# The last feed-forward of a hybrid trunk: block sums made in place, three steps begun ahead, fetches of hid in slots of their own

## The chip, the cores and the metric

One core of a Trainium2 chip runs the whole trunk in one launch. The metric is device time in microseconds (us): the median of several runs. One further execution is recorded by the hardware profiler; all rows of a profile come from it. Engines: PE is TensorE (matmul), PEld its weight loads, DVE is VectorE, ACT is ScalarE, POOL is GpSimd, SP is SyncE, which here only issues DMAs.

## The reference

Two layers of a mixing block (attention and a state-space scan) and a SwiGLU feed-forward, over 256 context and 1024 latent tokens, D_MODEL = 1024, float32. Only the feed-forward of the last layer is touched:

```python
f_l = rmsnorm(x_lat, norm_ffn_pre[l]) * (1.0 + sc2_l) + sh2_l
x_lat = x_lat + g2_l * rmsnorm(swiglu(f_l, w_gate[l], w_up[l], w_down[l]), norm_ffn_post[l])

def swiglu(h, w_gate, w_up, w_down):
    return (jax.nn.silu(h @ w_gate) * (h @ w_up)) @ w_down
```

In the last layer it is computed for the 1024 latent tokens alone. D_FF is 2816, 22 steps (`ff`) of 128.

## The kernel before

**Products.** Every float32 operand is held as a pair: hi, a rounded cast made on ACT (line 113), and lo, the difference made on POOL or DVE (line 114). `mm3` (lines 227 to 230) multiplies them in three matmuls of 128 x 128 x 512.

**The last feed-forward** (`ffn_last`) makes gate and up of one step together as a 2 x 2 block product with seven instead of eight multiplications (Strassen's scheme in Winograd's form). The weights' blocks of a step are A11, A12 (the halves of the gate's rows), A22 (a half of the up rows), and the sums S1 = u0 + u1, S2 = S1 - g0, S3 = g0 - u0, S4 = g1 - S2. The tokens' blocks are B11, B21, B22 and T1 to T4, made once by `quads` from the normalised tokens; B11 and B21 (tile `ha`) are there from the first half of the tokens, the others (`h_hb` holds T1 and T2, `h_hc` B22, `h_t` T3 and T4) need the second half, token tiles 6 to 9. One block's product is 12 matmuls, a step is 84. `head(ff)` makes A11·B11 and A12·B21, which need only `ha`; `rest(ff)` the other five, the sums in between on DVE, and stores the two halves of the hidden rows through an xt tile to DRAM (`hid`, line 1032).

**Weights.** `plan` lists the blocks in the order in which they are used, two to a ring slot `w_t`, five slots; `pump` fills a slot as soon as the one five places back is freed by TensorE. `wblock` (lines 201 to 224) makes one block: it fetches the step's gate or up weights (512 KB, line 208) into one of two raw slots (`raw_t`), makes the four sums (lines 217 to 220) into two xt tiles, and splits. Heads 0 and 1 are made before the second half of the tokens is there, so the gate weights of steps 0 and 1 are fetched twice. xt is a pool of six tiles of 128 x 1024 that tokens, quadrants, sums and hid share.

**The down projection** (`down_all`) takes the token tiles in groups of three, three and two (`GROUPS`), and for each group goes through all 22 steps: one weight block of 512 KB (line 124, cast and split as above, through the same raw slots and ring) and the hid rows of the group (line 1081, an xt tile of its own), 18 matmuls a step in the first two groups and 12 in the third. hid is fetched three steps ahead. A group's sums stay in PSUM (slots `ps_w`, five, and `ps_s`, three, of a bank each); at its end `finish_psum` and `postnorm` (lines 796 to 801) normalise them, add the residual, in xt tiles, and store.

**Order.** A scheduler, not the code's order alone, sets each engine's row of instructions when the kernel is built; at run time each engine goes through its own row in order and waits at an instruction until its operands and slots are there. SP issues all fetches of weights, tokens and hid in one row.

Of the kernel before, what the change touches and what calls it, by code (L numbers as in the profile page):

```python
# [9 lines left out]
F32 = mybir.dt.float32  # L10
F32R = mybir.dt.float32r
AF = mybir.ActivationFunctionType
ALU = mybir.AluOpType
# [4 lines left out]
P = 128  # L18
# [6 lines left out]
NCT = CTX // P  # L25
# [4 lines left out]
NFF = DFF // P  # L30
# [24 lines left out]
class Trunk:  # L55
# [73 lines left out]
    def plan(self):  # L129
# [15 lines left out]
        for l in range(DEPTH):  # L145
# [8 lines left out]
            if l == 1:  # L154
                flat = [(ff, b) for ff in range(2) for b in ("A11", "A12")]
                flat += [(ff, b) for ff in range(2) for b in ("S2", "S3", "S1", "A22", "S4")]
                flat += [(ff, b) for ff in range(2, NFF) for b in ("A11", "A12", "S2", "S3", "S1", "A22", "S4")]
# [42 lines left out]
    def wblock(self, w, ff, name):  # L200
# [11 lines left out]
        if name[0] == "S" and "S1" not in st:  # L212
            u = raw("u")
            a, b = self.x(), self.x()
            st["S1"], st["S2"], st["S3"], st["S4"] = a[:, 0:512], a[:, 512:1024], b[:, 0:512], b[:, 512:1024]
            add = nc.vector.tensor_tensor
            add(st["S1"], u[:, 0:512], u[:, 512:1024], op=ALU.add)
            add(st["S2"], st["S1"], g[:, 0:512], op=ALU.subtract)
            add(st["S3"], g[:, 0:512], u[:, 0:512], op=ALU.subtract)
            add(st["S4"], g[:, 512:1024], st["S2"], op=ALU.subtract)  # L220
        src = st[name] if name[0] == "S" else {"A11": g, "A12": g, "A22": st.get("u")}[name][:, 512 * (name != "A11"):512 * (name != "A11") + 512]
        self.split(w[:, 0], w[:, 1], src, nc.gpsimd)
        if name == ("A12" if ff < 2 else "S4"):
            st.clear()
# [736 lines left out]
    def quads(self, xs, i, B):  # L961
# [4 lines left out]
        for k2 in range(0, 4, 2):  # L966
# [13 lines left out]
            t3 = self.s2()  # L980
# [8 lines left out]
            tt(t3, b22, b12, op=ALU.subtract)  # L989
            tt(b12, b12, b11, op=ALU.subtract)  # L990
            put("T1", b12, nc.gpsimd)
            tt(b22, b22, b12, op=ALU.subtract)
            put("T2", b22, nc.vector)
            put("T3", t3, nc.vector)
            tt(b22, b22, b21, op=ALU.subtract)
            put("T4", b22, nc.gpsimd)

    def ffn_last(self, l, accp, xs0, xs1):
# [19 lines left out]

        def head(ff):
            a, x1, sa = self.psw(), self.s2(), self.s2()  # L1020
# [13 lines left out]
        def rest(ff):  # L1034
# [17 lines left out]
            p = self.psw()  # L1052
            mul(p, ff, "S4", "B22")
# [8 lines left out]
        self.quads(xs1, 1, B)  # L1062
        for ff in range(NFF):
            if ff > 1:
                head(ff)
            rest(ff)
        self.down_all(l)

    def down_all(self, l):
        nc = self.nc  # L1070
        loads = [(g, ff) for g in range(len(self.GROUPS)) for ff in range(NFF)]
        hx = {}

        def load(n):
            if n < len(loads):
                g, ff = loads[n]
                ts = self.GROUPS[g]
                w = len(ts) * P
                a = self.x(n=2 * w)
                o = (ts[0] - NCT) * P  # L1080
# [3 lines left out]
        for n in range(3):  # L1084
            load(n)
# [248 lines left out]
```

## Time and profile before

| what | value |
|---|---|
| runs | 3324.96, 3329.06, 3329.13 us, median 3329.06 |
| profiled execution | 3319.59 us, its span on the core 3317.8 |
| mean granted clock | 0.969 |
| last feed-forward, TensorE's part | from about 2564 to 3307 us of the span |
| down projection | from about 3034 to 3307 us |

The profiled execution is 9.5 us (0.28 %) shorter than the median of the runs. In rows of the profile "L208" is line 208 of the kernel, "raw_t<-in_w_up" the tile written and what is read, a number with x a count, and what stands in square brackets the idle time of the engine just ahead with what ended it.

### The profile page before, as it was taken

Reading aid. Unit: us, or ns where it says so; the run is one execution under the profiler, and the core shown is the slowest. Engines: PE = TensorE matmul, PEld = TensorE weight load, DVE = VectorE, ACT = ScalarE, POOL = GpSimd, SP = SyncE. Lnnn points to the kernel's source line nnn. Section 1 sums busy time; section 2 is a strip of 40 time slices with the busy share of each in tenths; the row PEclk is TensorE's granted clock in tenths of the full one; section 3 lists DMA queues with packets and bytes.
Section 4 is the critical chain, followed back from the end, with each engine's and each line's share of the span. In section 5 each row is a group of like instructions: output and inputs, shape, how many; then the busy total and the mean of one; then the engine's idle time right before and its main releaser. Section 6 shows DMA issues by size and latency. Waiting matters only on the chain. (4 is left out here: it accounts for less than half of the span.)

```text
span 3317.8 us, 44735 instructions
## 1 busy us (share of the span) xinstructions
PE 3097.4 (93%) x16411; PEld 2564.5 (77%) x16411; DVE 1722.2 (52%) x3188; ACT 1338.4 (40%) x2440; POOL 1546.7 (47%) x1429
## 2 busy tenths in 40 slices
PE   6999989999899999989999998889999699999997
PEld 4777768888777788866778787778887488887785
DVE  2657567765343344436334467677775655663000
ACT  4433347666422121134222354347675433332222
POOL 4226455444433223246344525644546655554665
PEclk8999889999999999999999999999999799999998
DMA  6376553221343322244444335752222333335766
GB/s 223 100 220 231 175 169 102 64 64 64 118 124 96 102 78 70 64 144 150 139 140 127 109 87 163 236 157 83 71 64 91 114 113 108 106 112 181 239 219 215
DMA packets 327082, 434.08 MB, mean 131 GB/s; under 512 B 22408, under 2 KB 236584, under 8 KB 326608
## 3 DMA queue, kind: packets, MB, share of 16 engines
q1 hardware_dynamic: 266976, 340.26, 33.5%
q10 hardware_dynamic: 59888, 90.97, 7.5%
q8 instruction: 130, 2.13, 0.3%
q14 instruction: 88, 0.72, 0.1%
HBM read 340.14 MB, written 91.01 MB: 130 GB/s over the span
## 5 line engine op out<-in xcount | busy, mean ns | idle before, releaser
L114 POOL TENSOR_TENSOR w_t<-raw_t,w_t 128x1024 fp32r<-128x1024 f32 (+2 forms) x288 | 619.5, 2156 | 916.2 <-ACT w_t L113 892.1
L113 ACT CAST w_t<-raw_t 128x1024 fp32r<-128x1024 f32 (+2 forms) x314 | 296.3, 949 | 682.0 <-PE ps_s L230 203.1
L1146 DVE TENSOR_TENSOR ffn_acc<-ffn_acc,ps_s 128x512 f32<-128x512 f32 x400 | 270.8, 685 | 201.0 <-PE ps_s L230 199.4
L848 DVE TENSOR_SCALAR_CACHE_REDUCE att_a<-ps_s 128x512 f32<-128x512 f32 (+1 forms) x400 | 226.9, 586 | 138.6 <-PE ps_s L847 128.2
L856 POOL TENSOR_SCALAR att_a<-att_a,att_st 128x1280 f32<-128x1280 f32 (+1 forms) x144 | 180.2, 1253 | 176.1 <-DVE att_st L855 109.5
L113 ACT CAST xt<-s2t 128x512 fp32r<-128x512 f32 (+2 forms) x148 | 80.6, 545 | 353.8 <-DVE s2t L1127 201.3
L228 PE MATMUL ps_s<-w_t,xt 128*128 128x512 f32 x528 | 211.6, 401 | 12.0 <-ACT xt L113 4.2
L1127 DVE TENSOR_TENSOR s2t<-s2t,ps_w 128x256 f32<-128x256 f32 (+1 forms) x66 | 39.4, 597 | 334.2 <-PE ps_w L230 318.5
L228 PE MATMUL ps_w<-ha,w_t 128*128 128x512 f32 x528 | 207.2, 394 | 1.9 <-ACT xt L979 1.1
L229 PE MATMUL ps_w<-ha,w_t 128*128 128x512 f32 x528 | 207.1, 393 | 1.7 <-DVE ha L387 1.7
L230 PE MATMUL ps_s<-w_t,xt 128*128 128x512 f32 x528 | 206.1, 393 | 1.5 <-DVE xt L114 1.5
L229 PE MATMUL ps_s<-w_t,xt 128*128 128x512 f32 x528 | 207.4, 393 | 0.0
L230 PE MATMUL ps_w<-ha,w_t 128*128 128x512 f32 x528 | 206.7, 392 | 0.0
L869 PE MATMUL ps_w<-cst_all,att_a 128*128 128x128 f32 x1312 | 198.5, 277 | 0.3 <-DVE xt L799 0.2
L854 ACT ACTIVATE att_a<-att_a,att_st 128x1280 f32<-128x1280 f32 (+1 forms) x144 | 183.2, 1273 | 37.2 <-DVE att_st L853 32.3
L114 POOL TENSOR_TENSOR w_t<-xt,w_t 128x512 fp32r<-128x512 f32 x88 | 127.3, 1457 | 111.4 <-ACT w_t L113 111.4
L799 DVE SCALAR_TENSOR_TENSOR xt<-ps_w,rstd_t,gate_row 128x512 f32<-128x512 f32 x48 | 33.6, 745 | 278.3 <-POOL rstd_t L236 278.2
L869 PEld LDWEIGHTS ps_w<-cst_all,att_a 128*128 128x128 f32 x1312 | 154.4, 142 | 11.3 <-DVE xt L799 5.4
L465 DVE SCALAR_TENSOR_TENSOR xt<-row,convw,xt 128x512 f32<-128x512 f32 (+1 forms) x128 | 126.4, 1041 | 68.8 <-ACT xt L463 51.3
L114 DVE TENSOR_TENSOR xt<-s2t,xt 128x512 fp32r<-128x512 f32 (+2 forms) x148 | 129.8, 877 | 49.3 <-ACT xt L113 47.9
L228 PE MATMUL ps_w<-hb,w_t 128*128 128x512 f32 x352 | 140.9, 400 | 0.8 <-ACT s2t L382 0.8
L229 PE MATMUL ps_w<-hb,w_t 128*128 128x512 f32 x352 | 139.5, 396 | 0.0
(334 smaller groups left out, 8551.5 us busy)
## 6 DMA issues: line engine op xcount, KB each, us to landing
raw_t<-in_w_down SPq DMA_DIRECT2D x110, 512.0 KB
raw_m<-in_w_mod SPq DMA_DIRECT2D x80, 512.0 KB
raw_t<-in_w_gate SPq DMA_DIRECT2D x68, 512.0 KB
raw_t<-in_w_up SPq DMA_DIRECT2D x66, 512.0 KB
hid<-xt ACTq DMA_DIRECT2D x44, 512.0 KB
xt<-xs SPq DMA_DIRECT2D x42, 512.0 KB
xt<-hid SPq DMA_DIRECT2D x44, 384.0 KB
raw_t<-in_w_in SPq DMA_DIRECT2D x32, 512.0 KB
```

The lines of the kernel that those rows point to most:

```text
L113: self.nc.scalar.copy(hi, src)
L114: (eng or self.nc.vector).tensor_tensor(lo, src, hi.bitcast(F32), op=ALU.subtract)
L228: mm(out, st[0], mv[0], start=first, stop=False)
L229: mm(out, st[0], mv[1], start=False, stop=False)
L230: mm(out, st[1], mv[0], start=False, stop=last)
L465: nc.vector.scalar_tensor_tensor(acc, row[:, o0 + k:o0 + k + n], cw[:, ct, k:k + 1], acc, op0=ALU.mult, op1=ALU.add)
L848: nc.vector.tensor_scalar(pb[:, j:j + m], s[:, :m], -0.125, None, op0=ALU.mult, op1=ALU.min, accum_out=st[:, n:n + 1])
L854: nc.scalar.activation(pb, pb, AF.Exp, bias=nmx, scale=-1.0, accum_out=st[:, 4:5])
L856: nc.gpsimd.tensor_scalar(pb, pb, st[:, 5:6], 1.0, op0=ALU.mult, op1=ALU.mult)
L869: nc.tensor.transpose(tp[:, (2 * k + h) * P:(2 * k + h + 1) * P], pr[h][:, (k2 + k) * P:(k2 + k + 1) * P], self.ident)
L1127: nc.vector.tensor_tensor(s, s, ps["u"][:, :n], op=ALU.mult)
L1146: nc.vector.tensor_tensor(acc[t][:, s], acc[t][:, s], p, op=ALU.add)
```

## The change

Three parts, all in the last feed-forward.

- **Sums in place.** S1 is written over u's first half, S2 and S4 over g's halves, and only S3 goes to a tile of its own (an s2 tile). No xt tile is used, but a gate slot is held until S2 and S4 are split, an up slot until S1 and A22 are. In `quads` the differences are made over B11, B12, B22 and B21; T1's lo is made on DVE and T3's on POOL, where it was the other way round.
- **Three steps begun.** head(2) stands ahead of the steps too, in two tiles of another pool, so the gate weights of step 2 are fetched a second time as well. Of step 0 the product S4·B22 is made first (`third`), copied to a tile x3 by ACT, and used later.
- **Fetches of hid.** The first three go to xt tiles and are issued ahead of the last step's `rest`; the others go to a ring of ten places in the space of `ha`, nine steps ahead.

The diff:

```diff
--- before.py
+++ after.py
@@ -152,9 +152,9 @@
             for kt in range(self.RING):
                 seq.append(((l, "o", kt), [(slice(0, 1024), I["w_out"][l][kt * P:(kt + 1) * P, :].unsqueeze(1))], (1, 1024)))
             if l == 1:
-                flat = [(ff, b) for ff in range(2) for b in ("A11", "A12")]
-                flat += [(ff, b) for ff in range(2) for b in ("S2", "S3", "S1", "A22", "S4")]
-                flat += [(ff, b) for ff in range(2, NFF) for b in ("A11", "A12", "S2", "S3", "S1", "A22", "S4")]
+                flat = [(ff, b) for ff in range(3) for b in ("A11", "A12")]
+                flat += [(ff, b) for ff in range(3) for b in (("S4",) if ff == 0 else ()) + ("S2", "S3", "S1", "A22") + (("S4",) if ff else ())]
+                flat += [(ff, b) for ff in range(3, NFF) for b in ("A11", "A12", "S2", "S3", "S1", "A22", "S4")]
                 self.wpos = {b: (i // 2, i % 2) for i, b in enumerate(flat)}
                 for i in range(0, len(flat), 2):
                     seq.append(((l, "w", i // 2), flat[i:i + 2], None))
@@ -211,16 +211,15 @@
         g = raw("g") if name in ("A11", "A12") or "S1" not in st else None
         if name[0] == "S" and "S1" not in st:
             u = raw("u")
-            a, b = self.x(), self.x()
-            st["S1"], st["S2"], st["S3"], st["S4"] = a[:, 0:512], a[:, 512:1024], b[:, 0:512], b[:, 512:1024]
+            st["S1"], st["S2"], st["S3"], st["S4"] = u[:, 0:512], g[:, 0:512], self.s2(), g[:, 512:1024]
             add = nc.vector.tensor_tensor
-            add(st["S1"], u[:, 0:512], u[:, 512:1024], op=ALU.add)
-            add(st["S2"], st["S1"], g[:, 0:512], op=ALU.subtract)
             add(st["S3"], g[:, 0:512], u[:, 0:512], op=ALU.subtract)
-            add(st["S4"], g[:, 512:1024], st["S2"], op=ALU.subtract)
+            add(st["S1"], st["S1"], u[:, 512:1024], op=ALU.add)
+            add(st["S2"], st["S1"], st["S2"], op=ALU.subtract)
+            add(st["S4"], st["S4"], st["S2"], op=ALU.subtract)
         src = st[name] if name[0] == "S" else {"A11": g, "A12": g, "A22": st.get("u")}[name][:, 512 * (name != "A11"):512 * (name != "A11") + 512]
         self.split(w[:, 0], w[:, 1], src, nc.gpsimd)
-        if name == ("A12" if ff < 2 else "S4"):
+        if name == ("A22" if ff == 0 else "S4") or name == "A12" and ff < 3:
             st.clear()
 
     def mm3(self, out, st, mv, first, last):
@@ -977,7 +976,6 @@
                     kt = k2 + 4 * half + k
                     o = half * 512 + k * 256
                     nc.scalar.activation(qb[:, o:o + 256], t[:, k * 256:(k + 1) * 256], AF.Identity, bias=cc[:, kt:kt + 1], scale=cc[:, 16 + kt:17 + kt])
-            t3 = self.s2()
             b11, b21, b12, b22 = qa[:, 0:512], qa[:, 512:1024], qb[:, 0:512], qb[:, 512:1024]
 
             def put(name, src, eng):
@@ -986,14 +984,14 @@
                 eng.tensor_tensor(d[:, :, 1], v(src), d[:, :, 0].bitcast(F32), op=ALU.subtract)
 
             put("B22", b22, nc.gpsimd)
-            tt(t3, b22, b12, op=ALU.subtract)
-            tt(b12, b12, b11, op=ALU.subtract)
-            put("T1", b12, nc.gpsimd)
-            tt(b22, b22, b12, op=ALU.subtract)
+            tt(b11, b12, b11, op=ALU.subtract)
+            tt(b12, b22, b12, op=ALU.subtract)
+            tt(b22, b22, b11, op=ALU.subtract)
             put("T2", b22, nc.vector)
-            put("T3", t3, nc.vector)
-            tt(b22, b22, b21, op=ALU.subtract)
-            put("T4", b22, nc.gpsimd)
+            put("T3", b12, nc.gpsimd)
+            put("T1", b11, nc.vector)
+            tt(b21, b22, b21, op=ALU.subtract)
+            put("T4", b21, nc.gpsimd)
 
     def ffn_last(self, l, accp, xs0, xs1):
         nc = self.nc
@@ -1016,8 +1014,16 @@
         tt = nc.vector.tensor_tensor
         st = {}
 
+        def third(ff):
+            p = self.psw()
+            mul(p, ff, "S4", "B22")
+            x3 = accp.tile([P, 512], F32, name="x3")
+            nc.scalar.copy(x3, p)
+            st["x3"] = x3
+
         def head(ff):
-            a, x1, sa = self.psw(), self.s2(), self.s2()
+            x1, sa = [accp.tile([P, 512], F32, name=f"head{i}") if ff == 2 else self.s2() for i in range(2)]
+            a = self.psw()
             mul(a, ff, "A11", "B11")
             nc.scalar.copy(x1, a)
             a = self.psw()
@@ -1049,8 +1055,11 @@
             tt(u3, u3, p, op=ALU.subtract)
             tt(sa, sa, u3, op=ALU.mult)
             emit_hid(sa, ff, 0)
-            p = self.psw()
-            mul(p, ff, "S4", "B22")
+            if ff == 0:
+                p = st["x3"]
+            else:
+                p = self.psw()
+                mul(p, ff, "S4", "B22")
             tt(u2, u2, p, op=ALU.add)
             nc.scalar.activation(u2, u2, AF.Silu)
             tt(u2, u2, x1, op=ALU.mult)
@@ -1060,28 +1069,44 @@
         self.quads(xs0, 0, B)
         head(1)
         self.quads(xs1, 1, B)
+        head(2)
+        third(0)
         for ff in range(NFF):
-            if ff > 1:
+            if ff > 2:
                 head(ff)
+            if ff == NFF - 1:
+                hx, load = self.hid_loader()
+                for n in range(3):
+                    load(n)
             rest(ff)
-        self.down_all(l)
-
-    def down_all(self, l):
-        nc = self.nc
-        loads = [(g, ff) for g in range(len(self.GROUPS)) for ff in range(NFF)]
-        hx = {}
+        self.down_all(l, hx, load)
+
+    def hid_loader(self):
+        self.loads = loads = [(g, ff) for g in range(len(self.GROUPS)) for ff in range(NFF)]
+        hx, ring = {}, []
 
         def load(n):
-            if n < len(loads):
-                g, ff = loads[n]
-                ts = self.GROUPS[g]
-                w = len(ts) * P
+            if n >= len(loads):
+                return
+            g, ff = loads[n]
+            ts = self.GROUPS[g]
+            w = len(ts) * P
+            if n < 3:
                 a = self.x(n=2 * w)
-                o = (ts[0] - NCT) * P
-                nc.sync.dma_start(a.rearrange("p (s n) -> p s n", s=2), self.hid_d[ff, :, :, o:o + w])
-                hx[n] = a.bitcast(F32R).rearrange("p (s n) -> p s n", s=2)
-
-        for n in range(3):
+            else:
+                if not ring:
+                    ring.append(self.big.tile([P, 8192], F32, tag="ha", name="hid_ring"))
+                at = (n % 10) * 768
+                a = ring[0][:, at:at + 2 * w]
+            o = (ts[0] - NCT) * P
+            self.nc.sync.dma_start(a.rearrange("p (s n) -> p s n", s=2), self.hid_d[ff, :, :, o:o + w])
+            hx[n] = a.bitcast(F32R).rearrange("p (s n) -> p s n", s=2)
+
+        return hx, load
+
+    def down_all(self, l, hx, load):
+        loads = self.loads
+        for n in range(3, 9):
             load(n)
         for n, (g, ff) in enumerate(loads):
             ts = self.GROUPS[g]
@@ -1096,7 +1121,7 @@
                 if ff == NFF - 1:
                     self.finish_psum(l, t, banks[i])
             self.free(l, "d", g, ff)
-            load(n + 3)
+            load(n + 9)
 
     def finish_psum(self, l, t, halves):
         if self.fgrow[0] != (l, 0):
```

Lines below are those of each kernel on its own; in the new one they are one or some twenty less or more (before's L969, L952, L796 are after's L968, L951, L795; L1081 is L1102).

At the beginning, SP, before: weight fetches (L208), tokens' fetches (L952, L796: residuals `xs`) and the quadrants of the first tokens (L969, from `hf`).

```order
L208 DMA raw_t<-in_w_gate 128x8x128
L208 DMA raw_t<-in_w_up 128x8x128
L208 DMA raw_t<-in_w_gate 128x8x128
L208 DMA raw_t<-in_w_up 128x8x128
L796 DMA xt<-xs_96 128x1024
L952 DMA xt<-xs_97 128x1024
L787 DMA gate_row<-mod_94 128x1024
L952 DMA xt<-xs_97 128x1024
L208 DMA raw_t<-in_w_gate 128x8x128
L969 DMA xt<-hf 128x512 x4
```

After:

```order
L795 DMA xt<-xs_96 128x1024
L208 DMA raw_t<-in_w_gate 128x8x128 x2
L208 DMA raw_t<-in_w_up 128x8x128
L951 DMA xt<-xs_97 128x1024
L786 DMA gate_row<-mod_94 128x1024
L951 DMA xt<-xs_97 128x1024
L968 DMA xt<-hf 128x512 x2
L208 DMA raw_t<-in_w_gate 128x8x128
L208 DMA raw_t<-in_w_up 128x8x128
L968 DMA xt<-hf 128x512 x6
```

The fetch of the third gate block has come in, and the last two token fetches (`xs_97`) stand ahead of one gate and one up fetch that were ahead of them.

At the beginning, POOL, before: scaling of `ha` (L386), splits (L114), and the normalising (L245, L235, L236) and scaling (L362) of token tiles.

```order
L386 TENSOR_SCALAR ha<-s2t 128x2x256 x3
L114 TENSOR_TENSOR w_t<-xt,w_t 128x512
L386 TENSOR_SCALAR ha<-s2t 128x2x256
L114 TENSOR_TENSOR w_t<-xt,w_t 128x512 x2
L114 TENSOR_TENSOR w_t<-raw_t,w_t 128x512
L114 TENSOR_TENSOR w_t<-xt,w_t 128x512 x4
L245 TENSOR_TENSOR ss_t<-ss_t 128x1
L235 TENSOR_SCALAR rstd_t<-ss_t 128x1
L236 TENSOR_TENSOR rstd_t<-rstd_t,mhalf 128x1
L362 TENSOR_SCALAR xt<-xt,rstd_t 128x1024
```

After (L385 is before's L386, L361 is L362, L244 is L245):

```order
L235 TENSOR_TENSOR rstd_t<-rstd_t,mhalf 128x1
L114 TENSOR_TENSOR w_t<-raw_t,w_t 128x512
L361 TENSOR_SCALAR xt<-xt,rstd_t 128x1024
L114 TENSOR_TENSOR w_t<-raw_t,w_t 128x512
L114 TENSOR_TENSOR w_t<-s2t,w_t 128x512
L114 TENSOR_TENSOR w_t<-raw_t,w_t 128x512
L244 TENSOR_TENSOR ss_t<-ss_t 128x1 x3
L114 TENSOR_TENSOR w_t<-raw_t,w_t 128x512
L234 TENSOR_SCALAR rstd_t<-ss_t 128x1 x3
L235 TENSOR_TENSOR rstd_t<-rstd_t,mhalf 128x1 x3
L361 TENSOR_SCALAR xt<-xt,rstd_t 128x1024 x3
L114 TENSOR_TENSOR w_t<-raw_t,w_t 128x512
```

Ahead of the last three scalings (L361 x3) there are now the five splits of step 0 (S2, S4, S3, S1, A22), the first of the four tiles scaled among them; before, the first tile was scaled after eight splits, and the next three followed without a split between.

At the beginning of the down projection, SP, before: weights (L124) and hid (L1081).

```order
L124 DMA raw_t<-in_w_down 128x1024 x6
L1081 DMA xt<-hid 128x2x384 x4
L124 DMA raw_t<-in_w_down 128x1024
L1081 DMA xt<-hid 128x2x384 x3
L124 DMA raw_t<-in_w_down 128x1024
L1081 DMA xt<-hid 128x2x384
```

After:

```order
L124 DMA raw_t<-in_w_down 128x1024 x3
L1102 DMA xt<-hid 128x2x384 x3
L1102 DMA hid_ring<-hid 128x2x384 x2
L124 DMA raw_t<-in_w_down 128x1024
L1102 DMA hid_ring<-hid 128x2x384 x8
L124 DMA raw_t<-in_w_down 128x1024 x2
L787 DMA xt<-in_norm_ffn_post 128x1024
L795 DMA xt<-xs_97 128x1024
L124 DMA raw_t<-in_w_down 128x1024 x2
L1102 DMA hid_ring<-hid 128x2x384
```

Three fetches of hid now stand behind three weight fetches, where four stood behind six, and ten more follow with one weight fetch among them.

On PE at the beginning, before: the end of head 1 (products with `ha`), the last transposes of the tokens (L975), then the first products S1·T1 (`h_hb`).

```order
L229 MATMUL ps_w<-ha,w_t 128x512
L230 MATMUL ps_w<-ha,w_t 128x512
L975 MATMUL ps_w<-cst_all,xt 128x128 x16
L228 MATMUL ps_s<-h_hb,w_t 128x512
L229 MATMUL ps_s<-h_hb,w_t 128x512
L230 MATMUL ps_s<-h_hb,w_t 128x512
L228 MATMUL ps_s<-h_hb,w_t 128x512
```

After (L974 is before's L975):

```order
L228 MATMUL ps_w<-ha,w_t 128x512
L229 MATMUL ps_w<-ha,w_t 128x512
L974 MATMUL ps_w<-cst_all,xt 128x128 x16
L227 MATMUL ps_w<-ha,w_t 128x512
L228 MATMUL ps_w<-ha,w_t 128x512
L229 MATMUL ps_w<-ha,w_t 128x512
L227 MATMUL ps_w<-ha,w_t 128x512
```

Behind the transposes there now stand head 2's 24 matmuls with `ha`, and behind those the products S4·B22 and S1·T1 of step 0 in turn; ahead of them head 1's 24 stand in one piece between two lots of 16 transposes, where before 4 and 12 transposes stood with head 1's products between and behind them.

## Prediction

> **What bounds the kernel now.** I read the page first (busy shares), then busy time by stretches of the last feed-forward, the waits of TensorE in the two stretches where it is not full, the rows around each wait, and last the chain that ended last.
>
> ```profile
> PE 3097.4 (93%) x16411; PEld 2564.5 (77%) x16411; DVE 1722.2 (52%) x3188; ACT 1338.4 (40%) x2440; POOL 1546.7 (47%) x1429
> ```
>
> TensorE is busy for 93 %: only its idle time, 220 us over the whole span, can be won, and the change touches the last 760 us alone. By stretches (start:end, length, busy us and count of PE, PEld, DVE, ACT, POOL, granted clock, DMA share, GB/s):
>
> ```profile
> 2580.00:2600.00 20.00, 10.21 (x44) 7.94 (x44) 8.52 (x7) 9.92 (x24) 14.66 (x20) 0.72 0.48 157
> 2600.00:2620.00 20.00, 6.67 (x19) 4.26 (x19) 15.61 (x16) 14.01 (x29) 14.89 (x10) 0.54 0.26 79
> 2900.00:2935.00 35.00, 35.00 (x155) 28.71 (x154) 20.60 (x28) 12.29 (x21) 17.07 (x13) 1.00 0.37 121
> 3100.00:3150.00 50.00, 43.26 (x180) 34.99 (x179) 7.16 (x7) 14.22 (x22) 35.15 (x23) 0.94 0.69 236
> 3250.00:3300.00 50.00, 47.10 (x203) 37.48 (x203) 0.00 (x0) 14.69 (x14) 31.09 (x13) 1.00 0.67 218
> ```
>
> The middle (third row) is full at clock 1.00: 35.00 / 155 = 0.226 us a matmul, so 2.71 us for a block's 12 and 19.0 us for a step's 84. Nothing can be won there. TensorE waits at the beginning and in the down projection:
>
> ```profile
> PE ps_w L975 <- POOL xt L362: 13.5, 2, 13.2
> PE ps_s L228 <- ACT h_hb L985: 6.2, 1, 6.2
> PE ps_w L228 <- DMA xt<-hid: 17.1, 3, 8.4
> PE ps_s L228 <- DVE xt L799: 2.4, 1, 2.4
> ```
>
> The first two are the beginning (2557 to 2640): the transposes of the last tokens wait for their scaling on GpSimd, and later the first product waits for its operand T1. The other two are the down projection: 17.1 us for fetches of hid, the hidden rows, in three waits, and 2.4 us for a PSUM bank.
>
> **The beginning.** The splits on GpSimd (a group of the page: busy us, mean ns of one), and rows of the beginning by time:
>
> ```profile
> L114 POOL TENSOR_TENSOR w_t<-xt,w_t 128x512 fp32r<-128x512 f32 x88 | 127.3, 1457 | 111.4 <-ACT w_t L113 111.4
> ...
> 2558.87 0.38 SPq L208 DMA_DIRECT2D raw_t<-in_w_up  x1
> 2573.87 0.37 SPq L208 DMA_DIRECT2D raw_t<-in_w_up  x1
> 2577.91 0.69 DVE L217 TENSOR_TENSOR xt<-raw_t 128x512 f32<-128x512 f32 x1 [2.96 <-DMA raw_t<-in_w_up]
> 2583.46 0.32 SPq L952 DMA_DIRECT2D xt<-xs  x1
> 2587.34 1.11 PE L975 MATMUL ps_w<-cst_all,xt 128*128 128x128 f32 x4 [13.17 <-POOL xt L362]
> 2591.71 1.13 POOL L362 TENSOR_SCALAR xt<-xt,rstd_t 128x1024 f32<-128x1024 f32 x1
> 2594.42 1.93 ACT L979 ACTIVATE xt<-ps_w,cols 128x256 f32<-128x256 f32 x4 [0.98 <-PE ps_w L975]
> 2622.21 0.63 PE L228 MATMUL ps_w<-h_t,w_t 128*128 128x512 f32 x1
> ```
>
> The chain: the fetch of token tile 7 stands on SP behind four weight fetches and behind a free xt slot, and goes out at 2583.46; its scaling on GpSimd ends at 2591.71 + 1.13 = 2592.84. From the first eviction (2594.42) the casts, sums and differences of the quadrants take 27.8 us until products run without a gap (2622.21).
>
> What changes, step by step. (1) No sums go to xt, so two xt slots a step are free and the fetches of tokens 6 and 7 stand ahead of ff 1's blocks; only the fetches of the third gate block and of ff 0's up block are ahead. In the new order the up block waits for the third gate block's splits: the old second fetch went out at 2558.87; the third gate block has the slot free at 2556.4 (its first fetch's place), lands 4.04 us after issue (2573.87 to 2577.91, the row of a like fetch), and its two splits end about 2564.7; so up goes out then, and tile 7 at about 2567 instead of 2583.5. (2) But GpSimd now has all five splits of ff 0 (S2, S4, S3, S1, A22) ahead of tile 7's scaling. Up lands at 2568.7; the four sums with the four differences of `ha` between them take about 9 us on VectorE, so S4 is there about 2578; the last of the five splits, at 1.46 us each, end about 2583 to 2584, the short work of three normalisations follows, and the scaling ends about 2587.2 instead of 2592.8. That is 5.6 us earlier, not the 16 that the fetch gains. (3) The 27.8 us from there I leave as they are: the sums made in place are as many (DVE's and GpSimd's counts don't change), T1's difference goes to VectorE and T3's to GpSimd. (4) The third head is 24 matmuls, 24 x 0.226 = 5.4 us, put where TensorE has 6.67 of 20 us busy (second row of the stretches); they are taken from behind the dense start, so the whole 5.4 us come off. The price is one 512 KB fetch more (the gate block is read again) and one copy of x3 on ScalarE, hidden in the idle 6 of 20 us that ScalarE has there. If that cover were gone it would be 0.6 us. (5) S4·B22 of ff 0 first gives TensorE 12 matmuls while T1 to T4 are made; they fill part of the same gap, and I count no more for them. Sum: 5.6 + 5.4 = 11.0. Ends: 4, if the splits hold tile 7 as late as before and only most of head 2 is hidden; 18, if the first wait of 13.2 falls almost whole.
>
> **The middle.** The up block's slot now comes free only after S1 and A22 are split, the gate's after S2 and S4. The loop per step is then: fetch 4.04, three sums of about 0.69 (2.1), cast 0.6, five splits of 1.46 (7.3): about 14 us against TensorE's 19.0. That hides it, with 5 us left each step and ten blocks split ahead. If the cover were gone, each microsecond over 19.0 would count about twenty times. I take 0, ends -1 and +2.
>
> **The down projection.** Three waits for hid, each followed by matmuls at a longer pitch (0.43 instead of 0.23):
>
> ```profile
> 3033.22 0.39 PE L229 MATMUL ps_w<-h_hc,w_t 128*128 128x512 f32 x1
> 3033.44 0.39 PE L230 MATMUL ps_w<-h_hc,w_t 128*128 128x512 f32 x1
> 3038.23 0.68 PE L228 MATMUL ps_w<-w_t,xt 128*128 128x512 f32 x1 [4.41 <-DMA xt<-hid]
> ...
> 3041.27 0.62 PE L229 MATMUL ps_w<-w_t,xt 128*128 128x512 f32 x1
> ...
> 3145.07 0.77 PE L228 MATMUL ps_w<-w_t,xt 128*128 128x512 f32 x1 [4.30 <-DMA xt<-hid]
> ...
> 3150.33 0.63 PE L228 MATMUL ps_s<-w_t,xt 128*128 128x512 f32 x1
> ...
> 3244.50 0.76 PE L228 MATMUL ps_w<-w_t,xt 128*128 128x512 f32 x1 [8.36 <-DMA xt<-hid]
> ```
>
> The first eight at 3038 take (3041.27 - 3038.23) / 7 = 0.43 us each, the thirteen at 3145 (3150.33 - 3145.07) / 12 = 0.44, and after the third wait it is twelve at the same pitch: 0.2 us too much each, 1.6, 2.6 and 2.4 us. So the waits cost 4.41 + 1.6 = 6.0, 4.30 + 2.6 = 6.9 and 8.36 + 2.4 = 10.8 us. The Trainium skill ("TensorE: Matmul & The Clock Gate", Part 1: The HAM clock gate) has TensorE fall to half clock after an idle window and come back after about 3.4 us of work, which by half of 3.4 would be an estimate of 1.7 us a wait, 5.1 for three; the trace has 6.6, and I use the trace.
>
> The cause of the first is the queue:
>
> ```profile
> 3008.45 23.82 SPq L124 DMA_DIRECT2D raw_t<-in_w_down  x5
> 3032.32 2.55 SPq L1081 DMA_DIRECT2D xt<-hid  x4
> ```
>
> The first hid fetch stands on SP behind six weight fetches, of which these five wait for raw slots until 3032. In the new order three hid fetches stand behind three weight fetches; at even spacing (23.82 / 5 = 4.8 us) the third of the six, the second of these five, goes out at 3013, and a step's slots held longer may add some 5 us, so the hid fetches go out 14 to 19 us earlier: 6.0 us gone. The other two waits are at the changes of token group, where the post-normalisation takes xt slots from a lookahead of three fetches; with slots of their own and nine ahead (9 x 18 x 0.226 = 37 us) the second, 6.9, goes too. What is late next there is the PSUM bank (2.4), which stays.
>
> The third is in the group of two tiles, 12 matmuls a step, 2.71 us, and there the weights are late next. The chain that ended last:
>
> ```profile
> 3240.52 5.69 DMA raw_t<-in_w_down
> ...
> 3246.25 4.83 issue
> ...
> 3253.54 4.03 DMA raw_t<-in_w_down
> ...
> 3257.67 1.06 ACT w_t L113
> ...
> 3303.09 2.41 POOL w_t L114
> ```
>
> From 3253.54 to the last split's end, 3303.09 + 2.41 = 3305.5, two raw slots in turn pass fetch, cast and split seven times: 52 / 7 = 7.4 us for two weight blocks, 3.7 each, against 2.71 that TensorE takes. So of the 10.8 us only the slack ahead of this loop can be won: the 4.83 in which the split stood ready, less 1.06 for the cast, is 3.8, and up to 1.7 more if the 5.69 us fetch takes 4.03 with fewer hid fetches beside it. I take 5.5 (ends 2 and 8). Sum of the down projection: 6.0 + 6.9 + 5.5 = 18.4, ends 8 and 22.
>
> **Sum.** 11.0 + 18.4 = 29.4 us. The profiled execution took 3319.59 us, 9.5 less than the median of the runs, 3329.06; it would come to 3290, and the median to 3329.06 - 29.4 = 3300.
>
> **Rivals.**
> - *The beginning gives nothing.* GpSimd is busy 14.66 of 20 us at 2580 to 2600 already, and the five splits move ahead of the scaling; with splits at 1.7 us and the sums waiting for up, tile 7 is as late as before, and head 2 only fills what was then filled by other products. For it: the first wait's releaser is GpSimd, not the fetch. Against: the fetch goes out 16 us earlier and head 2 needs none of it. Gain 18.4, time 3311. Chance 0.17.
> - *The hid fetches delay the weights.* Thirteen fetches of 384 KB now go out nearly at once, eight of them ahead of the fifth weight block on SP. At 236 GB/s (fourth row of the stretches) the eight take 3.1 MB / 236 = 13 us, and the ring's weights are needed one each 18 x 0.226 = 4.1 us from 3033.5 on. If the fifth weight block lands after 3050, TensorE waits, up to 10 us: 3310. Against: they start about 14 us before TensorE needs the first. The Trainium skill ("DMA: Bandwidth & Descriptors", Issuing engines are not separate DMA queues) says that all queues run on the same 16 engines and interleave, which speaks for this rival; no row of before has such a burst. Chance 0.12.
> - *Slower: the up block comes late in every step.* Its sums stand in VectorE's order ahead of the evictions of PSUM. The loop of about 14 us passes 19.0 if the fetch and its wait take 9 us instead of 4.04; every microsecond beyond costs 19 to 20, so from 10.6 us on the whole gain is spent, and at 12 us the time is about 3329 + 28 = 3357. For it: only two raw slots, and SP issues in order. Against: the DMA share is 0.37 in the middle, less than at the beginning (0.48), where a fetch took 4.04. Chance 0.07.
> - *Neither part bites:* the down projection's waits turn into weight waits and the beginning is unchanged, 3325 to 3330. Chance 0.04.
>
> **How the numbers follow.** My forecast, 3300, has 0.60, its own range 3288 to 3308 (the terms' ends, not all at once: 8 below the sum if the beginning gives 18, 12 above if it gives 4 and the last group 2). The first two rivals, both near 3311, have 0.29 and are taken into the range, and 6 us are left on the low side for runs that differ among themselves as 3324.96 and 3329.13 do: 3282 to 3316. What a measurement can tell from no change is 0.2 %, 6.7 us. Faster by more: 0.60 + 0.17 + 0.12 = 0.89; within: 0.04; slower: 0.07.
>
> **What would show it.** In the new profile the waits for hid are gone, and with them the pitch of 0.43 at 3038 and 3145; the last group's waits are for weights (L124's fetch, cast, split) with the loop at 7.4 us a pair; the transposes of the quadrants begin about 5 us earlier, and TensorE is dense about 5.6 us earlier with 24 matmuls more behind it; the middle stays at 0.226 us a matmul with no wait for a raw fetch. Wrong would make it: waits for weights in the first group's fifth to seventh steps, VectorE waiting for the up block in each step, or a first wait as long as now.

## The result, and the profile after

| | before | changed |
|---|---|---|
| median of 5 runs | 3329.13 us (3324.96 to 3331.1) | 3309.31 us (3299.49 to 3313.95) |
| ratio | | 0.994, 95 % interval 0.9919 to 0.996 |
| profiled execution, span | 3317.8 us | 3311.4 us |

The change makes the kernel faster by 19.8 us, 13 to 27 by the interval; 29.4 was forecast, 3300 us. In the new profile TensorE is busy for 94 % of the span, before for 93 %:

```profile
PE 3102.8 (94%) x16411; PEld 2566.6 (78%) x16411; DVE 1717.0 (52%) x3188; ACT 1336.4 (40%) x2441; POOL 1564.2 (47%) x1429
```

The two spans differ by 6.4 us only, because of something far from the change. First the rows of the first 400 us (before, then changed), in which both kernels do the same work in the same order:

```profile
0.00:400.00 400.00, 352.39 (x2014) 278.26 (x2015) 213.25 (x343) 156.77 (x305) 170.52 (x210) 0.95 0.59 191
```

```profile
0.00:400.00 400.00, 342.08 (x1943) 268.29 (x1944) 203.96 (x332) 152.86 (x297) 174.88 (x204) 0.94 0.58 186
```

TensorE has some 70 matmuls less done by then. Most of this delay (12 of 15.8 us) arose between 78 and 141 us, where weights are fetched, and it largely stays: the last product of the out-projection, up to which TensorE's row is the same in both kernels, is at 2557.11 us before and here at

```profile
2572.92 0.40 PE L229 MATMUL ps_w<-att_wo,xt 128*128 128x512 f32 x1
```

In the fourteen profiles of this study that place lies anywhere from 2553.5 to 2573.6, so I compare stages from it. One table for all kernels, each number a difference of two rows of that kernel's timeline. "Beginning and middle": from this last product to the first of the down projection, stall included; "down": from there to the end of the span; "last group": from the first normalising step (DVE) of the second token group to that of the third.

| kernel | out-projection ends | beginning and middle | down | last group | ratio of times (interval) |
|---|---|---|---|---|---|
| before | 2557.11 | 481.1 (476.7 without its 4.41 stall) | 279.6 (284.0 with it) | 78.0 | 1 |
| changed | 2572.92 | 468.6 | 269.8 | 74.8 | 0.994 (0.9919 to 0.996) |
| changed, again | 2564.38 | 466.0 | 269.2 | 76.4 | 0.9941 (0.992 to 0.9961) |
| ring alone (e1) | 2553.80 | 475.3 | 265.6 | 74.8 | 0.9955 (0.9938 to 0.9973) |
| no ring (e2) | 2553.52 | 472.0 (467.7 without its 4.31 stall) | 279.0 (283.3 with it) | 77.3 | 0.9987 (0.9975 to 0.9999) |
| splits on DVE (e4) | 2568.75 | 466.6 | 254.6 | 66.4 | 0.9903 (0.9887 to 0.9918) |
| four raw places (e5) | 2573.58 | 467.5 | 249.5 | 59.3 | 0.989 (0.9873 to 0.9908) |
| two heads (e6) | 2570.93 | 473.9 | 270.9 | 75.8 | 0.9972 (0.996 to 0.9983) |
| T1 on POOL (e7) | 2572.82 | 461.4 | 268.9 | 76.2 | 0.9919 (0.9902 to 0.9936) |
| S4·B22 not first (e8) | 2562.18 | 464.1 | 267.8 | 74.8 | 0.9909 (0.9894 to 0.9924) |
| step 1's sums on POOL (e9) | 2571.76 | 466.1 | 271.3 | 78.3 | 0.993 (0.9903 to 0.9956) |
| e5 + e7 + e8 (e10) | 2572.34 | 462.7 | 249.7 | 59.8 | 0.9882 (0.9858 to 0.9906) |
| e10, scaling on DVE (e11) | 2555.73 | 462.7 | 250.2 | 59.4 | 0.9879 (0.9856 to 0.9903) |
| e5 + e7 (e12) | 2567.68 | 462.0 | 249.1 | 59.2 | 0.9884 (0.9861 to 0.9907) |

Kernels with the same code in a stage agree within 3 to 4 us there, which is finer than the ratios; only e1's down projection lies further off, 2.2 us below the lowest of its like. By the stages the change brings 476.7 - 467.2 (mean of changed, again, e4 and e5) = 9.5 us ahead of the down projection and 284.0 - 269.5 = 14.5 in it. These 24.0 are 3 to 4 us more than the medians give (19.8, and 20.9 the second time). e1, which changes nothing ahead of the down projection, shows such a difference too (19.8 by the stages, 13.8 by the medians); a stage comes from one execution of each kernel, a median from several, and why the two differ was not found.

**The beginning after.** TensorE's waits there, then three stretches: the second is the one in which T1 to T4 are made, the third the middle.

```profile
PE ps_w L974 <- POOL xt L361: 8.0, 1, 8.0
PE ps_s L228 <- DVE h_hb L984: 6.3, 2, 3.4
```

```profile
2573.00:2604.00 31.00, 13.39 (x49) 9.96 (x48) 8.09 (x12) 14.51 (x36) 22.87 (x35) 0.70 0.63 204
2604.00:2640.00 36.00, 25.83 (x97) 20.20 (x96) 34.41 (x31) 25.21 (x47) 27.93 (x18) 0.79 0.25 74
2640.00:3041.00 401.00, 401.00 (x1754) 328.92 (x1753) 241.48 (x317) 141.50 (x245) 201.52 (x142) 1.00 0.37 120
```

The wait for the tokens' scaling fell from 13.2 to 8.0, but VectorE is now busy for 34.41 of 36.00 us, and the products S1·T1 wait for it (T1's lo is made there, L984). The middle is full, as before. VectorE, though, now waits there for the up block, 42.1 us in 20 steps (the last column is the idle time just ahead and what ended it), which costs TensorE nothing, as it has no wait in the middle:

```profile
L216 DVE TENSOR_TENSOR s2t<-raw_t 128x512 f32<-128x512 f32 x20 | 22.3, 1115 | 42.1 <-DMA raw_t<-in_w_up 42.1
```

**The down projection after.** It begins without a gap (3041.55 is its first matmul; pitch 0.23, where 0.43 stood). Its waits, SP's waits at the change from the first to the second token group, what SP issues there, and what ScalarE (casts) and GpSimd (splits) do:

```profile
PE ps_w L228 <- POOL w_t L114: 10.3, 12, 1.9
PE ps_w L227 <- ACT w_t L113: 1.2, 1, 1.2
```

```profile
3041.32 0.39 PE L229 MATMUL ps_w<-h_hc,w_t 128*128 128x512 f32 x1
3041.55 0.39 PE L227 MATMUL ps_w<-w_t,xt 128*128 128x512 f32 x1
```

```profile
SPq L1102 <- PE ps_s L229: 6.1, 4, 3.5
...
SPq L795 <- DVE xt L799: 4.7, 1, 4.7
```

```profile
3135.65 0.33 SPq L124 DMA_DIRECT2D raw_t<-in_w_down  x1
3140.80 0.32 SPq L795 DMA_DIRECT2D xt<-xs  x1
3144.65 4.14 SPq L1102 DMA_DIRECT2D hid_ring<-hid  x4
3148.90 2.31 SPq L124 DMA_DIRECT2D raw_t<-in_w_down  x2
```

```profile
3144.97 2.00 ACT L113 CAST w_t<-raw_t 128x1024 fp32r<-128x1024 f32 x2 [11.46 <-PE ps_s L229]
3146.10 4.74 POOL L114 TENSOR_TENSOR w_t<-raw_t,w_t 128x1024 fp32r<-128x1024 f32 x2 [1.54 <-ACT w_t L113]
3157.37 4.75 POOL L114 TENSOR_TENSOR w_t<-raw_t,w_t 128x1024 fp32r<-128x1024 f32 x2 [6.53 <-ACT w_t L113]
```

No wait for hid is left. But the weights fall behind at this change of groups: a weight fetch goes out 13 us after the one ahead (3135.65, 3148.90). SP issues in order, and ahead of this fetch a residual fetch (L795) waits 4.7 us for an xt tile and four hid fetches (L1102) wait 6.1 us for TensorE to leave their places in the ring. These waits delay it by 0.4 us at most, though, since it had no raw slot before: both slots held blocks whose casts waited 11.46 us for TensorE to leave a place of `w_t`, and the split that frees the first slot began at 3146.10 and takes 2.4 us, to about 3148.5. TensorE leaves the places late because from 3137.2 to 3143.8 it makes the next steps' products of the first two tiles alone (`ps_w`), and a place is free only behind the third tile's (`ps_s`). The weight fetch, beside the four hid fetches, then needs about 7.3 us until its cast begins (3156.24), GpSimd stands idle for 6.53 us, and the weights, ahead by few blocks, catch up no more. In the last group the chain is the one of before, fetch, cast and split in two slots:

```profile
3251.41 4.60 DMA raw_t<-in_w_down
...
3256.11 1.06 ACT w_t L113
...
3257.24 2.39 POOL w_t L114
...
3288.36 3.21 DMA raw_t<-in_w_down
```

From 3251.41 to 3288.36 five rounds, 7.4 us each, for two blocks: what it was before.

### The profile page after: what moved, and what is told of

Read it like the earlier page. It is cut to its first block, busy times and chain, and to the rows that moved or that the text cites. A ratio compares the mean times of both kernels' runs of the same rounds, so it can differ in the third digit from the quotient of the medians.

```text
span 3311.4 us, 44759 instructions
## 1 busy us (share of the span) xinstructions
PE 3102.8 (94%) x16411; PEld 2566.6 (78%) x16411; DVE 1717.0 (52%) x3188; ACT 1336.4 (40%) x2441; POOL 1564.2 (47%) x1429
## 4 chain that ended last, share of the span: by engine, by line
PE 41%; DVE 4%; DMA 3%; POOL 3%; issue 2%; ACT 2%; ACTq 0%; SPq 0%; POOLq 0%; DVEq 0%
PE ps_w L227 7%; PE ps_w L228 7%; PE ps_w L229 7%; PE ps_s L227 4%; PE ps_s L228 4%; PE ps_s L229 4%; PE ps_w L875 2%; PE ps_w L868 2%; PE ps_s L846 2%; POOL w_t L114 1%; DMA raw_t<-in_w_down 1%; ACT w_t L113 1%; PE ps_w L278 0%; DMA xt<-xs 0%; PE ps_w L731 0%
## 5 line engine op out<-in xcount | busy, mean ns | idle before, releaser
L114 POOL TENSOR_TENSOR w_t<-raw_t,w_t 128x1024 fp32r<-128x1024 f32 (+2 forms) x354 | 733.0, 2079 | 1005.9 <-ACT w_t L113 983.5
L113 ACT CAST w_t<-raw_t 128x1024 fp32r<-128x1024 f32 (+2 forms) x380 | 334.6, 891 | 709.4 <-DMA raw_t<-in_w_down 201.8
L227 PE MATMUL ps_s<-w_t,xt 128*128 128x512 f32 x446 | 180.0, 404 | 9.5 <-ACT xt L113 4.4
L228 PE MATMUL ps_s<-w_t,xt 128*128 128x512 f32 x446 | 175.8, 394 | 0.0
L229 PE MATMUL ps_s<-w_t,xt 128*128 128x512 f32 x446 | 174.4, 394 | 1.4 <-DVE xt L114 1.4
L114 DVE TENSOR_TENSOR xt<-s2t,xt 128x512 fp32r<-128x512 f32 (+2 forms) x147 | 144.6, 984 | 43.5 <-ACT xt L113 41.4
L227 PE MATMUL ps_w<-hb,w_t 128*128 128x512 f32 x352 | 140.9, 400 | 1.5 <-ACT s2t L381 1.5
L228 PE MATMUL ps_w<-hb,w_t 128*128 128x512 f32 x352 | 139.6, 397 | 0.0
L229 PE MATMUL ps_w<-hb,w_t 128*128 128x512 f32 x352 | 139.4, 396 | 0.0
```

The costliest lines, as they stand in the source:

```text
L113: self.nc.scalar.copy(hi, src)
L114: (eng or self.nc.vector).tensor_tensor(lo, src, hi.bitcast(F32), op=ALU.subtract)
L227: mm(out, st[0], mv[0], start=first, stop=False)
L228: mm(out, st[0], mv[1], start=False, stop=False)
L229: mm(out, st[1], mv[0], start=False, stop=last)
```

## The experiments

**e1, e2: the ring alone, and all but the ring.** e1 is the kernel before with this edit (shortened here; `hid_loader` as in the diff of the change); e2 is the changed kernel with it undone.

```diff
-        self.down_all(l)
+            if ff == NFF - 1:          # ahead of the last rest(ff)
+                hx, load = self.hid_loader()
+                for n in range(3):
+                    load(n)
+        self.down_all(l, hx, load)     # load(n + 9), ring of ten in "ha"
```

> The kernel before with one part of the change alone: the first three hid fetches ahead of the last step and the ring of ten places. Theory A (the down projection's gain of about 14 us in the two profiles comes from the fetches of hid having places of their own): 13 to 17 us faster than before, ratio about 0.9955; from the first matmul of the down projection's place to the end of the span about 270 us, as in the changed kernel, against 284 before. Theory B (it needs the xt tiles that the sums in place set free, since the first three fetches still go to xt): the first wait for hid stays, 6 us less gain, ratio about 0.9975.

> The changed kernel with the down projection's fetches of hid as before (three ahead, in xt tiles). Theory A: only the beginning's gain is left, 8 us by the two profiles, ratio about 0.9975, and three waits for hid come back. Theory B (freed xt tiles alone take away the waits at the changes of token group): ratio 0.995 or less, and one or two of the waits stay away.

e1 took 0.9955 (13.8 us less by the medians, 3310.32 against 3324.08), and its down projection 265.6 us: theory A, and the ring needs no freed xt tile; the first wait is gone too. e2 shows the other half:

```profile
PE ps_w L227 <- DMA xt<-hid: 16.3, 3, 7.7
PE ps_w L228 <- POOL w_t L114: 3.5, 5, 1.3
PE ps_s L227 <- DVE xt L798: 2.4, 1, 2.4
```

These are the three waits of before (17.1 us in 3) and its PSUM wait (2.4), so theory B falls. 9.0 us are left ahead of the down projection by the stages; by the times the ratio is 0.9987, 4.5 us, with theory A's 0.9975 at the end of its interval. The two halves act apart: by the medians 13.8 and 4.5 are 18.3 of the change's 19.8.

**e4, e5: what bounds the last group.** e4 splits its weights on VectorE, e5 fetches the weights of the second and third groups into four places of the space of T1 and T2.

Shortened:

```diff
-... or key[2:] == (0, 0) else self.nc.gpsimd)
+... or key[2:] == (0, 0) or key[:3] == (1, "d", 2) else self.nc.gpsimd)      # e4
```

```diff
+            r = self.raw_ring[:, 1024 * place:1024 * place + 1024]   # e5: raw_ring in "hb",
-        r = self.raw.tile([P, 1024], F32, tag="raw", name="raw_t")   # place = block % 4
```

> The changed kernel, the weights of the last token group (12 matmuls a step) split on VectorE instead of GpSimd. Theory A (that group is bound by fetch, cast and split through two raw slots, 7.1 us for two blocks): a split of 2.4 us becomes 1.3 to 1.4, the loop 6.0 us a pair, 15 blocks times 0.5 us: 7 to 8 us faster than the changed kernel, about 3301, ratio about 0.992. Theory B (bound by the fetches' bandwidth or by hid): within 2 us of the changed kernel, ratio 0.994.

> The changed kernel, the weight fetches of the second and third token groups in four places of the space that T1 and T2 held, instead of in the two raw slots. Theory A (the last group waits for the two slots): fetches overlap, the rate is GpSimd's 2.4 us a block, below TensorE's 2.71, so the last group takes about 60 instead of 77 us: 13 to 17 us faster than the changed kernel, about 3294, ratio 0.9895. Theory B (the fetches' bandwidth bounds: 768 KB a step at 260 GB/s is 3.0 us): about 8 to 11 us, ratio 0.991. Theory C (neither): no gain, 0.994.

e4: 3291.7 us, 0.9903. The chain of it, a round now 6.4 and 5.7 us:

```profile
3249.91 3.93 DMA raw_t<-in_w_down
...
3255.02 1.24 DVE w_t L114
...
3256.28 3.30 DMA raw_t<-in_w_down
...
3262.01 4.78 DMA raw_t<-in_w_down
```

e5: 3286.99 us, 0.989, the last group 59.3 us, and its stretch (60 us from 3221) is full:

```profile
3221.00:3281.00 60.00, 59.69 (x263) 48.94 (x262) 7.60 (x8) 21.57 (x29) 48.80 (x29) 1.00 0.71 250
```

22 x 2.71 is 59.6: TensorE itself bounds now, and in the whole down projection it has no wait. Theory A in both; theory B of e5 falls, since TensorE waits for nothing. By the stages e5 wins 20 us, 3 more than its theory gave: the last group 15 to 17, as expected, and the second group the rest. e4 won about 15 us by the stages where 7 to 8 were expected: the second group gains too (its first normalising step comes at 179.3 us of the down projection instead of 183.5 and 185.8). In the changed kernel TensorE waits for weights at that group's end (1.9 and 1.2 us in the first profile); in e4 it doesn't. Where the rest of these 4 to 7 us comes from was not looked into.

**e6 to e9: the beginning.** e6 begins two steps ahead, e7 puts T1's lo on GpSimd, e8 leaves S4·B22 of step 0 at its old place, e9 makes step 1's four sums on GpSimd. Shortened:

```diff
-        flat = [(ff, b) for ff in range(3) ...        # e6, and head(2) left out
+        flat = [(ff, b) for ff in range(2) ...
-            put("T1", b11, nc.vector)                 # e7
+            put("T1", b11, nc.gpsimd)
-        third(0)                                      # e8, S4 last in step 0's blocks
-            add = nc.vector.tensor_tensor             # e9
+            add = (nc.gpsimd if ff == 1 else nc.vector).tensor_tensor
```

> The changed kernel with two steps begun ahead instead of three (the third gate block isn't read twice; S4·B22 of step 0 still first). Measured by the time from the last product of the out-projection to the first of the down projection, 468.6 us in the changed kernel, 466.6 and 467.5 in two others with the same code there. Theory A (head 2's 24 matmuls fill idle time of TensorE): 5.4 us more, 473. Theory B (the time is set by VectorE, on which T1 and T2 wait, and head 2 only delays): 468 or less, since the gate block's two splits and the one 512 KB fetch fall away.

> The changed kernel with the lo parts of T1 on GpSimd (as before) and T3 on GpSimd (as changed): four subtractions less on VectorE, which is busy for 34.4 of 36 us while T1 to T4 are made. Theory A (VectorE sets the beginning): 4 x 1.2 = about 5 us less from the out-projection to the down projection, 463. Theory B (GpSimd, busy 27.9 of those 36 us, gets four of 1.7 more and becomes the bound): within 1.5 us of 467.6, or more.

> The changed kernel without S4·B22 of step 0 first: it comes at its old place. Theory A (its 12 matmuls fill gaps in which TensorE waits for T1): up to 2.7 us more, 470. Theory B (those gaps aren't filled by it, because its operand B22 is split as late): 467.6 within 1 us.

> The changed kernel with step 1's four sums on GpSimd instead of VectorE, where they stand (3.6 us) ahead of the quadrants' differences. Theory A (VectorE sets the beginning): about 3.5 us less, 464. Theory B (GpSimd gets four additions at 1.5 us or more and delays the splits and T3, T4): 467.6 or more.

e6: 473.9, 6.7 more than the mean of 467.2: head 2 is worth about what was forecast (5.4). Not all of the 6.7 need be its own, since in e6 the scheduler also puts head 0 later on TensorE, behind a wait of 17.9 us for `ha`. e7: 461.4, 5.8 less: VectorE set the beginning. Its stretch shows the two engines even, 29.56 and 29.67 of 33.00:

```profile
2600.00:2633.00 33.00, 25.57 (x99) 20.51 (x100) 29.56 (x24) 24.35 (x45) 29.67 (x20) 0.82 0.21 65
```

e8: 464.1, 3.1 less than the mean and 1.9 less than the lowest of its like, against both theories: by this one profile S4·B22 first costs time. The scaling of token tiles 6 and 7 in e8, and of 7 to 9 in the changed kernel (its tile 6 comes at 2592.73):

```profile
2585.42 2.22 POOL L361 TENSOR_SCALAR xt<-xt,rstd_t 128x1024 f32<-128x1024 f32 x2
```

```profile
2602.14 3.75 POOL L361 TENSOR_SCALAR xt<-xt,rstd_t 128x1024 f32<-128x1024 f32 x3
```

Tile 7's scaling ends 25.5 us behind the out-projection in e8 (2585.42 + 2.22 - 2562.18), against 30.3 in the changed kernel's first profile and 27.6 in its second. With S4 first, five of step 0's splits stand ahead of it on GpSimd instead of four, and they stand behind the first tile's normalisation, for which GpSimd is idle for 5.5 us (4.4 in the second profile). Of these 2 to 5 us 3.1 are left; VectorE is nearly full next (34.35 of 36.00 us busy in e8 too). e9: 466.1, between its two theories and within the spread of 466.0 to 468.6: no verdict.

**e10 to e12: together.** e10 is e5 with e7 and e8, e12 e5 with e7, e11 e10 with the last four tiles scaled on VectorE.

> The changed kernel with three edits of the experiments together: four raw places for the weights of the second and third token groups, T1's lo on GpSimd, and S4·B22 of step 0 at its old place. Theory A (the beginning's two edits act in different places, the splits ahead of the tokens' scaling and VectorE's row): from the out-projection to the down projection 467.6 - 6.2 - 3.5 = 458, down projection 249.5, some 28 us less than the changed kernel in the profile, about 3281 by the median, ratio 0.9855. Theory B (both relieve the same row of VectorE): 461 us, 3284, ratio 0.9865.

> The kernel of the three edits, with the last four token tiles scaled on VectorE instead of GpSimd, ahead of which GpSimd has the splits. Theory A (those splits hold the scaling back): the scaling comes 3 to 5 us earlier, 455 us or less from the out-projection to the down projection. Theory B (VectorE then gets four instructions of 1 us or more in the row that sets the beginning): no gain or 2 us lost against the three edits.

> The changed kernel with four raw places and T1's lo on GpSimd, S4·B22 first as changed. 461 us from the out-projection to the down projection and 249.5 behind it: about 3286 by the median, ratio 0.987; theory A of the three edits puts this one 3 to 4 us behind them, theory B within 1 us.

> The changed kernel once more, beside the others on the same chip. If the 15.8 us by which its first profile reached the end of the out-projection later than the kernel before belong to the run and not to the change: this time between 2553 and 2574 again without order, 467.6 us within 1.5 from there to the down projection, 269 within 2 behind it, ratio 0.994 within 0.002.

e10 and e12 are alike (462.7 and 462.0), which is theory B's number: e8's edit adds nothing once T1's lo is on GpSimd. By the profiles, though, the row that takes the gain is GpSimd's rather than VectorE's, which theory B named. Tile 7's scaling ends 3.7 us earlier in e10 than in e12 (24.0 against 27.7 behind the out-projection), but GpSimd is then busy for 33.43 of 35.00 us while T1 to T4 are made, and the products of T1 wait for it (3.3 us). e11 neither gains nor loses: TensorE's wait for the scaling is 3.1 instead of 4.3 us, and the wait for T1 on GpSimd stays. In e11:

```profile
PE ps_s L234 <- POOL h_hb L990: 3.3, 1, 3.3
...
PE ps_w L980 <- DVE xt L367: 3.1, 1, 3.1
```

GpSimd's stretch in e10:

```profile
2597.00:2632.00 35.00, 24.64 (x91) 19.01 (x89) 31.37 (x24) 24.67 (x45) 33.43 (x23) 0.79 0.24 76
```

All three beat both kernels, 3282 to 3286 us against 3323.32 before on the same chip, ratio 0.988 (0.9856 to 0.991); e12 with two edits is as good as any. The changed kernel again gave 0.9941 and the out-projection's end at 2564.38, and e2, with the same code up to there, 2553.52: the 15.8 us of its first profile belong to the execution.

## Why the prediction was right, and where its sizes were off

The sign, the places and the range (3282 to 3316) held; the gain was two thirds of what was forecast. The forecast's own range, 3288 to 3308, has its two sides exchanged: 8 us below and 12 above 3300 are 3292 to 3312, and only that holds 3309.31. As a number, 3309.31 is as near to the first two rivals (3311 and 3310). It is the stages that decide against them: the beginning gave 9.5 us where the first rival has nothing, and TensorE has no wait for weights in the first group, where the second has up to 10. By its steps:

- **Tile 7 earlier (5.6 us).** The last scaling of the pair that TensorE waits for ended at 2592.84 - 2557.11 = 35.7 us from the out-projection's end, now TensorE's transposes behind it start at 2603.32 - 2572.92 = 30.4: 5.3, and 8.0 in the second profile (27.7). The steps towards it held as well: tile 7's fetch goes out 10.2 us behind the out-projection (2583.07), where 26.4 stood (2583.46), 16 us earlier as forecast, and GpSimd's splits stand ahead of the scaling.
- **Head 2 (5.4 us).** e6 gives 6.7, not all of it surely head 2's.
- **"The 27.8 us from there I leave as they are."** This step failed. From the first eviction (2604.26) to dense products (2639.49, the first with `h_t`) it is 35.2 us, and 34 in the second profile, so dense products begin 1.5 us later than before (2.2 earlier in the second), not 5.6 earlier. T1's lo went to VectorE, which the step booked as a swap without a price; e7, with T1's lo and T3's both on GpSimd, prices these four subtractions on VectorE at 5.8 (the swap itself was not run). VectorE's instructions with two SBUF operands also take longer beside GpSimd, which the count of instructions doesn't show (below).
- **S4·B22 first, "I count no more for them".** By e8's one profile a loss of 3.1 in the change as it is; with T1's lo on GpSimd (e10 against e12) none. What it costs lies in the order of splits ahead of the scaling; the second step counts S4's split there, but not as a price of this product. What it gives is hidden in the sum: 36 products of 128x512 more are done when TensorE begins to run densely (92 against 56), 8.1 us, of which the forecast counted head 2's 24, 5.4. So the sum of the beginning came out near, 8.1 in the first profile and 9.5 in the mean against 11.0, partly by luck: a step that failed by 7 us was offset by products that were counted for nothing and, in the later profiles, by tile 7.
- **The middle, 0.** 401.00 of 401.00 us busy. VectorE does wait for the up block in every step (42.1 us in 20), which the prediction named as a sign of being wrong; but the blocks split ahead cover it, and the slower rival's loss didn't occur. No run tried how near it is.
- **First wait for hid, 6.0.** The first group ends 91.2 us after the down projection's first matmul, where before it was 92.9 + 4.41 = 97.3 after the matmul could have begun: 6.1. The Trainium skill ("TensorE: Matmul & The Clock Gate", Part 1: The HAM clock gate) gives about 3.4 us of work at half clock behind an idle window, by which an estimate of the loss is half of that, 1.7 us; the trace of before had 1.6, and both are within what this row can tell.
- **Second wait, 6.9; PSUM wait stays, 2.4.** The second group took 99.8 before, 94.6 and 91.6 in the two profiles of the changed kernel: 5 to 8, where the second wait alone was to give 6.9. The PSUM wait went, against the forecast: with hid further ahead, TensorE's row takes later steps' products of the first two tiles before the third tile's (3137.2 to 3143.8), which covers it. The same order holds the places of `w_t` longer, and at the group's end TensorE waits for weights (1.9 and 1.2 us).
- **Third wait, 5.5.** Mis-sized: 78.0 to 74.8 and 76.4, so 1.6 to 3.2. The bound (7.4 us a pair of blocks) was named rightly; the error was to let it begin in the last group. Without the waits for hid TensorE reaches that group earlier by more than the weights do: their last split ends 257.14 us after the down projection's first matmul, before 267.25 + 4.41 = 271.66, and it is this 14.5, not the sum of the waits (18.4), that the down projection gained.
- **The rival that hid fetches delay the weights** was looked for at the start, where it doesn't occur. At the change of groups it occurs in a weak form: the order on SP costs a weight fetch 0.4 us at most, and beside four hid fetches it takes 7.3 us. What holds the weights there is that the two raw slots stay full while the casts wait for places of `w_t`. e5 has the same order on SP (four hid fetches ahead of a weight fetch at 3148.41) and the same wait of its casts (11.37 us), and with four raw places, more of them fetched by then, it is free of waits. Open is why e1's down projection is 4 us shorter than the changed kernel's.

## What to carry to other kernels

When a wait goes, price the stage by what feeds it next: follow the slowest supply (here two raw slots, 3.7 us a block) from the stage's beginning, since waits that TensorE no longer makes were also time in which the supply caught up. An instruction that goes to the engine whose results are waited for isn't a swap, even if the counts stay. Fetches that wait for a place stand ahead of all that is behind them in the same queue: before, five weight fetches held hid back until 3032.32, and e1 won the 4.41 us by issuing hid ahead of them. But before a late fetch is put down to its queue, look whether it had a place to go to: the weight fetch at 3148.90 stood behind four waiting fetches, and its own slot came free only at about 3148.5.

## What the runs showed of the hardware

A subtraction of 128x512 on VectorE takes 0.68 us alone and up to 1.78 beside GpSimd, and the one that reads PSUM doesn't stretch:

```profile
2615.30 1.64 DVE L993 TENSOR_TENSOR xt<-xt 128x512 f32<-128x512 f32 x1
2616.86 0.68 DVE L1031 TENSOR_TENSOR s2t<-s2t,ps_w 128x512 f32<-128x512 f32 x1
...
2618.55 1.78 DVE L989 TENSOR_TENSOR xt<-xt 128x512 f32<-128x512 f32 x1
```

While the changed kernel makes T1 to T4, the ones that GpSimd's work doesn't overlap take 0.68 or 0.69 and those wholly overlapped 1.00 to 1.78. The Trainium skill ("SBUF — State Buffer", SBUF: two separate sides) says that VectorE with two SBUF inputs and GpSimd share a pair of ports that one of them holds for a whole instruction; the traces agree, and the PSUM row fits it. The same split of 128x1024 takes 2.4 us on GpSimd and 1.24 on VectorE (e4). And the end of the same, untouched work spread over 20 us in the fourteen profiles (2553.5 to 2573.6), as much as the change is worth.
